# High part first in every weight-stationary stage, and two changes of place in the down-projections

## The chip, the cores and the metric

The kernel runs on 1 core of one Trainium2 chip. The metric is the device time of one execution in microseconds (us). Before the change it is 592.21 us, the median of 3 runs (592.15 to 592.26).

## The reference, cut to what matters

A decoder trunk of two layers works on one sequence of 256 positions with a width of 1024, all in float32. Layer 0 mixes with an mLSTM, layer 1 with a block-sparse attention on shared keys and values; behind each mixer stands a convolutional feed-forward block, and it is there that most of the products are:

```python
def conv_ffn(x, norm_g, w_up, conv_w, conv_b, w_down):
    u = rmsnorm(x, norm_g) @ w_up                  # 1024 -> 5632
    up = jnp.pad(u, ((0, 0), (CONV_W - 1, 0), (0, 0)))
    c = conv_b + up[:, 0:s_] * conv_w[0]
    for j in range(1, CONV_W):                     # 3 taps along the sequence
        c = c + up[:, j:j + s_] * conv_w[j]
    val, gate = jnp.split(c, 2, axis=-1)           # 2816 each
    return (jax.nn.silu(gate) * val) @ w_down      # 2816 -> 1024
```

## The kernel before, in words

Activations lie transposed: 128 channels on the partitions, 256 positions along the free axis. Every number that enters a product is split in two float32r parts, a high part `hi` (a rounded copy, made by ScalarE) and a low part `lo` (the rest, made by VectorE as raw minus `hi`). A product of x and w is taken as w_hi·x_hi + w_hi·x_lo + w_lo·x_hi.

**The weight-stationary step.** `steps_w` (L226) makes products whose weights are the stationary operand. For each k (a block of 128 input channels) it issues two matmuls into one PSUM bank: the *high* one, 128x128 weights from `hi` against 512 columns (x_hi and x_lo side by side in one tile, `both[k]`), and the *low* one, weights from `lo` against the 256 columns of x_hi. In what follows a pair of these is called a step; it has 768 columns. The order within a step is a parameter: with `order="h"` the high matmul comes first, with `order="l"` the low one does, except at k = 0. TensorE runs its instructions in the order in which the program writes them (L86); the other engines' orders are set by a planner.

**Where `steps_w` is used, in order of time.**
- `kq_steps` (L547): 8 outputs of 8 steps each, order l; the first two are taken in turns with a gate matmul (L556).
- `project_out` (L301), once a layer: 8 outputs of 8 steps, order l. The first four outputs are done in two halves of k, since the second half of the operand comes late.
- The up-projection (`pair`, L359), once a layer: 22 weight tiles (i), each with two outputs of 8 steps. Tiles 0 and 1 go ahead in turns, order l. For the others L387 chooses: layer 0, i = 2 to 11: order h, the two outputs one after the other; layer 0, i = 12 to 21: order l, in turns; layer 1, i = 2 to 11: order h, "side" (both high matmuls of a k, then both low ones); layer 1, i = 12 to 21: order h, in turns.
- The down-projection (`down`, L393), once a layer: 8 outputs of 22 steps each, 176 steps; order h in layer 0, l in layer 1. The last output of layer 1 takes its high matmul in two of 256 columns (`apart=False`).

**Weights.** `unit` (L155) loads one tile by one DMA into `raw`, and splits it in two equal pieces. `raw` has 3 buffers, `hi` and `lo` have 4 each, all of 2048 elements a partition. A tile of the up-projection holds 16 blocks of 128 columns, so the k of one output are 1024 bytes apart; a tile of the down-projection holds 11, and its k are 512 bytes apart, on end.

**Places.** Operand tiles are 2048 bytes a partition each. In the program before, those called `xa` and `xb` (the operands of all other stages) begin 1152 bytes behind a multiple of 2048, those called `f` (the 22 operands of a down-projection, made in `finish`) 256 bytes behind one. All `hi` and `lo` tiles begin 128 bytes behind a multiple of 2048. The `f` tiles are the first in their pool; four kinds of small tiles (`xs`, `y`, `sg`, `a`) lie behind them.

Of the kernel before, what the change touches and what calls it, by code (L numbers as in the profile page):

```python
# [11 lines left out]
F32 = mybir.dt.float32  # L12
# [6 lines left out]
P = 128  # L19
D = 1024  # L20
S = 256
# [48 lines left out]
def mix(steps, items=()):  # L70

    items, now = list(items), 0.0
    for cost, step in steps:
        while items and items[0][0] <= now:
            items.pop(0)[1]()
        step()
        now += cost
    for _, item in items:
        item()
# [3 lines left out]
def yoco_kernel(ctx: ExitStack, tc: tile.TileContext, A, out):  # L83
# [20 lines left out]
    @contextmanager  # L104
    def lend(label, name):
        with tc.tile_pool(name=label, bufs=2, reuse_waits="tile", space=bass.MemoryType.PSUM) as p:
            ring[name].insert(0, (p, 2))
            turns[name] = 0
            yield
            ring[name].pop(0)  # L110
            turns[name] = 0
# [43 lines left out]
    def unit(src, length, pieces=PIECES):  # L155
# [7 lines left out]
            nc.vector.tensor_tensor(lo[:, c], raw[:, c], hi[:, c].bitcast(F32), OP.subtract)  # L163
        return hi, lo

    def split(hi, lo, src, g=None):
        if g is None:
            return (nc.scalar.activation(hi, src, AF.Copy),
                    nc.vector.tensor_tensor(lo, src, hi.bitcast(F32), OP.subtract))  # L169
        return (nc.scalar.activation(hi, src, AF.Copy, scale=g),  # L170
                nc.vector.scalar_tensor_tensor(lo, src, g, hi.bitcast(F32), op0=OP.mult, op1=OP.subtract))  # L171
# [13 lines left out]
    def operand(pool, name, n):  # L185
        ts = [pool.tile([P, 2 * S], F32R, name=f"{name}{k}") for k in range(n)]
        return [t[:, :S] for t in ts], [t[:, S:] for t in ts], ts
# [35 lines left out]
            nc.scalar.activation(self.rB, pb[:, :S], AF.Copy)  # L223


    def steps_w(ps, w, at, x, ks, kall, done=None, apart=True, order="l", part="hl"):  # L226


        xh, xl, both = x

        def one(k):
            (hi, lo), p = w(), ps()
            c = slice(at(k), at(k) + P)
            last = k == kall - 1
            first = k == 0 or order == "h"

            def high():
                if not apart:
                    for n, xs in enumerate((xh, xl)):
                        nc.tensor.matmul(p[:, :S], hi[:, c], xs[k], start=k == 0 and n == 0,  # L240
                                         stop=last and not first and n == 1)
                    return
                nc.tensor.matmul(p, hi[:, c], both[k], start=k == 0, stop=last and not first)  # L243

            if first and "h" in part:
                high()
            if "l" in part:
                nc.tensor.matmul(p[:, :S], lo[:, c], xh[k], start=False, stop=last and first)  # L248
            if not first:
                high()  # L250
            if last and done is not None:
                done(p)

        return [(0.32, lambda k=k: one(k)) for k in ks]
# [37 lines left out]
    def residual(n, ps, gains, apart=True):  # L292
        nc.vector.tensor_tensor(hT[:, n], ps[:, :S], hT[:, n], OP.add)
        if apart:
            nc.vector.tensor_tensor(hT[:, n], ps[:, S:], hT[:, n], OP.add)
        if gains is None:
            nc.sync.dma_start(out[:, n, :], hT[:, n])
        else:
            feed(n, gains)
# [16 lines left out]
    def conv_ffn(l, gains):  # L316
        r = Rstd()
        with tc.tile_pool(name=f"ffn{l}", bufs=1, reuse_waits="tile") as fp, \
                tc.tile_pool(name=f"ffw{l}", bufs=2, reuse_waits="tile") as fw, lend(f"ffp{l}", "acc"):
            act = operand(fp, "f", KF)  # L320
            ah, al, _ = act

            def conv(ps, c, scaled):
                u = whole(ps)
                if not scaled:
                    nc.vector.tensor_tensor(u, u, r.rB, OP.mult)
                w = [par[:, C_CW + (l * 3 + j) * 2 * KF + c:][:, :1] for j in range(3)]
                b = par[:, C_CB + l * 2 * KF + c:][:, :1]
                y = fw.tile([P, S], F32, name="y", bufs=4)
                nc.scalar.activation(y, u, AF.Identity, bias=b, scale=w[2])  # L330
                for j in (1, 0):
                    d = 2 - j
                    nc.vector.scalar_tensor_tensor(y[:, d:], u[:, :S - d], w[j], y[:, d:],  # L333
                                                   op0=OP.mult, op1=OP.add)
                return y

            def finish(i, ps):
                y = [conv(ps[half](), half * KF + i, i >= DEFER) for half in range(2)]
                sg = fw.tile([P, S], F32, name="sg", bufs=2)
                nc.scalar.activation(sg, y[1], AF.Silu)  # L340
                a = fw.tile([P, S], F32, name="a", bufs=2)
                nc.gpsimd.tensor_tensor(out=a, in0=sg, in1=y[0], op=OP.mult)  # L342
                nc.scalar.activation(ah[i], a, AF.Copy)  # L343
                nc.gpsimd.tensor_tensor(out=al[i], in0=a, in1=ah[i].bitcast(F32), op=OP.subtract)  # L344

            def rescale():

                r.row()
                g0 = C_FNORM + l * KD
                for k in range(KD):  # L350
                    xs = fw.tile([P, S], F32, name="xs", bufs=4)
                    new = (nc.vector.scalar_tensor_tensor(xs, hT[:, k], par[:, g0 + k:g0 + k + 1], r.rB,
                                                          op0=OP.mult, op1=OP.mult),
                           nc.scalar.activation(setB[0][k], xs, AF.Copy))
                    if k == KD // 2 - 1:
                        half.extend(new)
                    nc.gpsimd.tensor_tensor(out=setB[1][k], in0=xs, in1=setB[0][k].bitcast(F32), op=OP.subtract)

            def pair(i, ks, order="l", turns=False):  # L359
                x = setA if i < DEFER else setB  # L360
                st = [steps_w(ps[i][half], w[i], lambda k, half=half: k * 256 + half * P, x, ks, KD, order=order)
                      for half in range(2)]
                if turns == "side":
                    parts = [[steps_w(ps[i][half], w[i], lambda k, half=half: k * 256 + half * P, x, ks, KD,
                                      order="h", part=part) for half in range(2)] for part in ("h", "l")]
                    return [s for k in range(len(ks)) for part in parts for s in (part[0][k], part[1][k])]
                return [s for both in zip(*st) for s in both] if turns else st[0] + st[1]


            w = [Once(lambda i=i: unit(A["w_up"][l, i], 2048)) for i in range(KF)]  # L370
            w[AHEAD] = Once(lambda: behind(last, lambda: unit(A["w_up"][l, AHEAD], 2048)))
            w[AHEAD + 1] = Once(lambda: behind(half, lambda: unit(A["w_up"][l, AHEAD + 1], 2048)))
            half = []
            ps = [[Once(acc) for half in range(2)] for i in range(KF)]


            late = []
            steps = []
            for k in range(KD):
                new = [s for i in range(AHEAD) for s in pair(i, [k])]  # L380
                steps += new[:-1] + late
                late = new[-1:]
            mix(steps + late, [(3.0, r.sums), (5.0, rescale)])
            for i in range(AHEAD):
                finish(i, ps[i])
            for i in range(AHEAD, KF):
                mix(pair(i, range(KD), *((("h", False), ("l", True)), (("h", "side"), ("h", True)))[l][i // 12]))  # L387
                finish(i, ps[i])

            wd = [Once(lambda i=i: unit(A["w_down"][l, i], 11 * P)) for i in range(2 * KD)]  # L390
            pd = [Once(acc) for n in range(KD)]

            def down(n, ks):  # L393
                apart = gains is not None or n < KD - 1
                return [s for k in ks for s in
                        steps_w(pd[n], wd[2 * n + k // 11], lambda q: (q % 11) * P, act, [k], KF,
                                lambda p: residual(n, p, gains, apart), apart, "h" if l == 0 else "l")]


            for ks in (range(KF // 2), range(KF // 2, KF)):  # L400
                for n in range(HOLD):
                    mix(down(n, ks))
            for n in range(HOLD, KD):
                mix(down(n, range(KF)))
# [509 lines left out]
```

## Time and profile before

| | |
|---|---|
| median of 3 runs | 592.21 us |
| the profiled execution's own time | 591.4 us |
| its span, first to last instruction | 589.7 us |
| TensorE busy | 583.8 us, 99% of the span |
| VectorE busy | 486.9 us, 83% |
| ScalarE busy | 393.4 us, 67% |
| GpSimd busy | 164.6 us, 28% |
| granted TensorE clock | 1.0 (the 2.4 GHz level) throughout |

The profile is of one execution. PE is TensorE's matmuls, PEld its weight loads, DVE VectorE, ACT ScalarE, POOL GpSimd. A matmul's recorded duration overlaps that of its neighbours, so the time that a matmul takes of its stage is read from one start to the next, or from the length of a stretch over the matmuls in it.

### The profile page before, as it was taken

The page shows a single profiled execution, that of the slowest core. Times are in us where ns is not written, and L with a number is a line of the kernel's source. Part 1 is how long each engine was busy: PE and PEld are TensorE (multiplying, and loading weights), DVE is VectorE, ACT ScalarE, POOL GpSimd, SP SyncE. Part 2 cuts the span into 40 slices and gives each one's busy share as a digit, 9 for nine tenths or more (in the row PEclk, how much of TensorE's full clock was granted, in tenths as well). Part 3 has the DMA queues.
Part 4 walks back from the last instruction along what each step waited for, and adds up shares of the span by engine and source line. Part 5 has one row for each costly group of instructions (what it writes and reads, how often), then busy time and mean ns, then how long its engine had stood idle before and what let it go on. Part 6 is the DMA issues. An engine that isn't in the chain of part 4 may idle for free.

```text
span 589.7 us, 9006 instructions
## 1 busy us (share of the span) xinstructions
PE 583.8 (99%) x3266; PEld 503.5 (85%) x3266; DVE 486.9 (83%) x843; ACT 393.4 (67%) x731; POOL 164.6 (28%) x178
## 2 busy tenths in 40 slices
PE   8999999999999999999999999999999999999997
PEld 5888888888888888888888888888888888888887
DVE  6888677799999998788867787577999999988550
ACT  6777776486786785775666687646887778776330
POOL 3001301352455444401211110025335343431000
PEclk9999999999999999999999999999999999999999
DMA  8657434347544544476745533333554645446720
GB/s 292 240 218 272 143 142 149 138 157 272 204 153 162 197 169 124 153 264 223 265 163 217 200 124 140 127 132 131 188 203 182 214 148 210 147 149 212 235 98 18
DMA packets 18620, 105.77 MB, mean 179 GB/s; under 512 B 2320, under 2 KB 3856, under 8 KB 9104
## 3 DMA queue, kind: packets, MB, share of 16 engines
q1 hardware_dynamic: 18288, 104.68, 49.8%
q10 hardware_dynamic: 288, 0.52, 0.3%
q8 instruction: 25, 0.41, 0.3%
q14 instruction: 19, 0.16, 0.1%
HBM read 104.15 MB, written 1.05 MB: 178 GB/s over the span
## 4 chain that ended last, share of the span: by engine, by line
PE 98%; DMA 1%; DVE 0%; SPq 0%; ACT 0%; issue 0%
PE acc L243 48%; PE acc L248 25%; PE acc L265 6%; PE acc L267 6%; PE acc L266 6%; PE acc L240 1%; DMA hT<-xT 1%; PE mis L643 1%; PE mis L761 1%; PE acc L771 1%; PE mis L815 0%; PE mis L789 0%; PE acc L770 0%; PE mis L816 0%; PE mis L675 0%; PE mis L610 0%
## 5 line engine op out<-in xcount | busy, mean ns | idle before, releaser
L163 DVE TENSOR_TENSOR lo<-raw,hi 128x1024 fp32r<-128x1024 f32 (+1 forms) x210 | 235.5, 1155 | 23.0 <-ACT hi L162 22.6
L243 PE MATMUL acc<-xb,hi 128*128 128x512 f32 x736 | 250.4, 394 | 0.0
L162 ACT ACTIVATE hi<-raw 128x1024 fp32r<-128x1024 f32 (+1 forms) x210 | 193.1, 968 | 44.2 <-PE acc L243 22.2
L248 PE MATMUL acc<-xb,lo 128*128 128x256 f32 x736 | 190.2, 279 | 0.0
L243 PEld LDWEIGHTS acc<-xb,hi 128*128 128x128 f32 x736 | 131.4, 188 | 23.6 <-DVE xb L171 0.2
L248 PEld LDWEIGHTS acc<-xb,lo 128*128 128x128 f32 x736 | 138.6, 188 | 8.4
L243 PE MATMUL acc<-f,hi 128*128 128x512 f32 x330 | 115.5, 393 | 0.0
L333 DVE SCALAR_TENSOR_TENSOR y<-whole,par,y 128x254 f32<-128x254 f32 (+1 forms) x176 | 100.3, 605 | 2.1 <-ACT y L330 1.4
L248 PE MATMUL acc<-f,lo 128*128 128x256 f32 x352 | 98.2, 283 | 0.0
L342 POOL TENSOR_TENSOR a<-sg,y 128x256 f32<-128x256 f32 x44 | 59.5, 1354 | 104.7 <-ACT sg L340 104.6
L243 PEld LDWEIGHTS acc<-f,hi 128*128 128x128 f32 x330 | 61.6, 188 | 13.7
L248 PEld LDWEIGHTS acc<-f,lo 128*128 128x128 f32 x352 | 66.1, 188 | 0.6
L330 ACT ACTIVATE y<-whole,par 128x256 f32<-128x256 f32 x88 | 51.1, 594 | 11.4 <-DVE whole L286 7.7
L243 PE MATMUL acc<-xa,hi 128*128 128x512 f32 x160 | 55.7, 395 | 1.0 <-DVE xa L171 1.0
L265 PE MATMUL acc<-hi,xa 128*128 128x512 f32 x128 | 52.6, 411 | 0.0
L344 POOL TENSOR_TENSOR f<-a,f 128x256 fp32r<-128x256 f32 x44 | 42.2, 959 | 31.3 <-ACT f L343 31.2
L267 PE MATMUL acc<-hi,xa 128*128 128x512 f32 x128 | 50.2, 392 | 0.0
L266 PE MATMUL acc<-lo,xa 128*128 128x512 f32 x128 | 50.0, 390 | 0.0
L199 POOL TENSOR_TENSOR sqacc<-sqacc,sq 128x256 f32<-128x256 f32 x18 | 16.1, 897 | 105.4 <-ACT sq L198 105.2
L248 PE MATMUL acc<-xa,lo 128*128 128x256 f32 x160 | 42.7, 284 | 0.3 <-DVE lo L169 0.3
L343 ACT ACTIVATE f<-a 128x256 fp32r<-128x256 f32 x44 | 18.2, 414 | 32.0 <-POOL a L342 32.0
L286 DVE TENSOR_TENSOR whole<-acc,whole 128x256 f32<-128x256 f32 x89 | 35.1, 413 | 3.3 <-ACT whole L285 3.3
(198 smaller groups left out, 664.4 us busy)
## 6 DMA issues: line engine op xcount, KB each, us to landing
raw<-w_up SPq DMA_DIRECT2D x44, 1024.0 KB, 4.8
raw<-w_down SPq DMA_DIRECT2D x32, 704.0 KB, 4.1
raw<-w_kqv SPq DMA_DIRECT2D x12, 1024.0 KB, 4.8
raw<-w_vo SPq DMA_DIRECT2D x8, 1024.0 KB, 5.2
raw<-w_out SPq DMA_DIRECT2D x4, 1024.0 KB, 4.7
raw<-w_o SPq DMA_DIRECT2D x4, 1024.0 KB, 4.8
raw<-w_kq SPq DMA_DIRECT2D x2, 1024.0 KB, 8.0
raw<-w_kq SPq DMA_DIRECT2D x2, 512.0 KB, 6.4
```

The costliest lines, as they stand in the source:

```text
L162: nc.scalar.activation(hi[:, c], raw[:, c], AF.Copy)
L163: nc.vector.tensor_tensor(lo[:, c], raw[:, c], hi[:, c].bitcast(F32), OP.subtract)
L243: nc.tensor.matmul(p, hi[:, c], both[k], start=k == 0, stop=last and not first)
L248: nc.tensor.matmul(p[:, :S], lo[:, c], xh[k], start=False, stop=last and first)
L265: nc.tensor.matmul(p, xh[k][:, ts], hi[:, c], start=k == 0, stop=False)
L266: nc.tensor.matmul(p, xh[k][:, ts], lo[:, c], start=False, stop=False)
L267: nc.tensor.matmul(p, xl[k][:, ts], hi[:, c], start=False, stop=k == KD - 1)
L286: nc.vector.tensor_tensor(y, ps[:, :S], y, OP.add)
L330: nc.scalar.activation(y, u, AF.Identity, bias=b, scale=w[2])
L333: nc.vector.scalar_tensor_tensor(y[:, d:], u[:, :S - d], w[j], y[:, d:], op0=OP.mult, op1=OP.add)
L342: nc.gpsimd.tensor_tensor(out=a, in0=sg, in1=y[0], op=OP.mult)
L344: nc.gpsimd.tensor_tensor(out=al[i], in0=a, in1=ah[i].bitcast(F32), op=OP.subtract)
```

## The change

`steps_w` loses the parameters `order` and `part`: the high matmul always comes first. `pair` loses its turns: the two outputs of a tile always follow each other. Layer 0 gets a tile of 224 floats (896 bytes) that nothing uses in front of the `f` tiles, so that these begin 1152 bytes behind a multiple of 2048. In layer 1 a new function `unit_down` makes the weights of the down-projection: blocks 0 to 7 of a tile go to its even places, blocks 8 to 10 to places 1, 3 and 5; consecutive k are then 1024 bytes apart, and the two pieces are of 8 and 3 blocks in place of 5.5 each.

```diff
+    def unit_down(src):
+        raw = wraw.tile([P, 2048], F32, name="raw")[:, :11 * P]
+        nc.sync.dma_start(raw, src)
+        hi, lo = (wsp.tile([P, 2048], F32R, name=nm) for nm in ("hi", "lo"))
+        for odd, a, b in ((0, 0, 8), (1, 8, 11)):
+            h, l = (w.rearrange("p (s e c) -> p s e c", s=8, e=2)[:, :b - a, odd] for w in (hi, lo))
+            r = raw.rearrange("p (s c) -> p s c", s=11)[:, a:b]
+            nc.scalar.activation(h, r, AF.Copy)
+            nc.vector.tensor_tensor(l, r, h.bitcast(F32), OP.subtract)
+        return hi, lo
...
-    def steps_w(ps, w, at, x, ks, kall, done=None, apart=True, order="l", part="hl"):
+    def steps_w(ps, w, at, x, ks, kall, done=None, apart=True):
...
-            first = k == 0 or order == "h"
-            def high():
-                ...
-            if first and "h" in part:
-                high()
-            if "l" in part:
-                nc.tensor.matmul(p[:, :S], lo[:, c], xh[k], start=False, stop=last and first)
-            if not first:
-                high()
+            if apart:
+                nc.tensor.matmul(p, hi[:, c], both[k], start=k == 0, stop=False)
+            else:
+                for n, xs in enumerate((xh, xl)):
+                    nc.tensor.matmul(p[:, :S], hi[:, c], xs[k], start=k == 0 and n == 0, stop=False)
+            nc.tensor.matmul(p[:, :S], lo[:, c], xh[k], start=False, stop=last)
...
+            if l == 0:
+                fp.tile([P, 224], F32, name="pad")
             act = operand(fp, "f", KF)
...
-                mix(pair(i, range(KD), *((("h", False), ("l", True)), (("h", "side"), ("h", True)))[l][i // 12]))
+                mix(pair(i, range(KD)))
...
-            wd = [Once(lambda i=i: unit(A["w_down"][l, i], 11 * P)) for i in range(2 * KD)]
+            even = l == 1
+            wd = [Once(lambda i=i: unit_down(A["w_down"][l, i]) if even else unit(A["w_down"][l, i], 11 * P))
+                  for i in range(2 * KD)]
+            def place(k):
+                q = k % 11
+                return (q if not even else 2 * q if q < 8 else 2 * q - 15) * P
...
-                        steps_w(pd[n], wd[2 * n + k // 11], lambda q: (q % 11) * P, act, [k], KF,
-                                lambda p: residual(n, p, gains, apart), apart, "h" if l == 0 else "l")]
+                        steps_w(pd[n], wd[2 * n + k // 11], place, act, [k], KF,
+                                lambda p: residual(n, p, gains, apart), apart)]
```

## Rows read from the trace of the kernel before

**Rows 1.** The page: span, TensorE's busy time, granted clock by slices.

```profile
span 589.7 us, 9006 instructions
PE 583.8 (99%) x3266; PEld 503.5 (85%) x3266; DVE 486.9 (83%) x843; ACT 393.4 (67%) x731; POOL 164.6 (28%) x178
...
PEclk9999999999999999999999999999999999999999
```

**Rows 2.** The page: chain that ended last, by engine and by line.

```profile
PE 98%; DMA 1%; DVE 0%; SPq 0%; ACT 0%; issue 0%
PE acc L243 48%; PE acc L248 25%; PE acc L265 6%; PE acc L267 6%; PE acc L266 6%; PE acc L240 1%; DMA hT<-xT 1%; PE mis L643 1%; PE mis L761 1%; PE acc L771 1%; PE mis L815 0%; PE mis L789 0%; PE acc L770 0%; PE mis L816 0%; PE mis L675 0%; PE mis L610 0%
```

**Rows 3.** Up-projections by stretch: window, its length, PE busy (matmuls touching it), clock, DMA.

```profile
127.86:177.78 49.92, 49.92 (x290) 1.00 0.57 208
177.78:233.74 55.96, 55.96 (x322) 1.00 0.47 165
413.12:468.87 55.75, 55.75 (x322) 1.00 0.54 190
468.87:524.33 55.46, 55.46 (x322) 1.00 0.50 176
```

**Rows 4.** Output projections (second four outputs), same view.

```profile
99.31:110.50 11.19, 11.19 (x65) 1.00 0.54 187
390.08:401.26 11.18, 11.18 (x65) 1.00 0.49 188
```

**Rows 5.** Order of time in the first stage: start, length, engine, line, idle before.

```profile
8.94 0.40 PE L556 MATMUL acc<-xa,hi 128*128 128x512 f32 x1
9.63 0.38 PE L248 MATMUL acc<-xa,lo 128*128 128x256 f32 x1 [0.29 <-DVE lo L169]
9.85 0.40 PE L243 MATMUL acc<-xa,hi 128*128 128x512 f32 x1
10.08 0.28 PE L248 MATMUL acc<-xa,lo 128*128 128x256 f32 x1
...
8.88 0.69 DVE L169 TENSOR_TENSOR lo<-raw,hi 128x512 fp32r<-128x512 f32 x1
...
8.23 0.62 ACT L168 ACTIVATE hi<-raw 128x512 fp32r<-128x512 f32 x1
```

**Rows 6.** The late operand of the first output projection, VectorE and TensorE.

```profile
94.20 0.48 DVE L171 SCALAR_TENSOR_TENSOR xb<-mis,par,xb 128x256 fp32r<-128x256 f32 x1 [0.54 <-ACT xb L170]
...
94.55 0.28 PE L248 MATMUL acc<-xb,lo 128*128 128x256 f32 x1
94.74 0.50 PE L243 MATMUL acc<-xb,hi 128*128 128x512 f32 x1
95.08 0.28 PE L248 MATMUL acc<-xb,lo 128*128 128x256 f32 x1
```

**Rows 7.** Down-projections by stretch: layer 0; layer 1 without its last output.

```profile
233.74:295.53 61.79, 61.79 (x354) 1.00 0.65 226
524.33:578.37 54.04, 54.04 (x311) 1.00 0.50 164
```

**Rows 8.** TensorE's order of time: layer 0 down-projection, then layer 1 up-projection in turns.

```profile
251.64 0.40 PE L243 MATMUL acc<-f,hi 128*128 128x512 f32 x1
251.88 0.28 PE L248 MATMUL acc<-f,lo 128*128 128x256 f32 x1
252.00 0.39 PE L243 MATMUL acc<-f,hi 128*128 128x512 f32 x1
252.22 0.28 PE L248 MATMUL acc<-f,lo 128*128 128x256 f32 x1
252.34 0.40 PE L243 MATMUL acc<-f,hi 128*128 128x512 f32 x1
252.58 0.28 PE L248 MATMUL acc<-f,lo 128*128 128x256 f32 x1
252.70 0.40 PE L243 MATMUL acc<-f,hi 128*128 128x512 f32 x1
...
502.84 0.40 PE L243 MATMUL acc<-xb,hi 128*128 128x512 f32 x1
503.07 0.28 PE L248 MATMUL acc<-xb,lo 128*128 128x256 f32 x1
503.19 0.39 PE L243 MATMUL acc<-xb,hi 128*128 128x512 f32 x1
```

**Rows 9.** Forms of the two splitting instructions on ACT and DVE, and of one strided write.

```profile
L163 DVE TENSOR_TENSOR lo<-raw,hi 128x1024 fp32r<-128x1024 f32 x146 | 180.9, 1267 | 11.3 <-ACT hi L162 10.9
L163 DVE TENSOR_TENSOR lo<-raw,hi 128x704 fp32r<-128x704 f32 x64 | 54.6, 897 | 11.7 <-ACT hi L162 11.6
L629 DVE SCALAR_TENSOR_TENSOR V<-acc,rc,V 128x512 fp32r<-128x512 f32 x4 | 3.0, 748 | 0.8 <-ACT V L628 0.8
```

**Rows 10.** Splits of two down-projection tiles, TensorE's use of them; VectorE busy.

```profile
242.70 1.70 DVE L163 TENSOR_TENSOR lo<-raw,hi 128x704 fp32r<-128x704 f32 x2 [0.20 <-ACT hi L162]
...
245.56 0.28 PE L248 MATMUL acc<-f,lo 128*128 128x256 f32 x1
...
533.90 2.23 DVE L163 TENSOR_TENSOR lo<-raw,hi 128x704 fp32r<-128x704 f32 x2
...
541.86 0.28 PE L248 MATMUL acc<-f,lo 128*128 128x256 f32 x1
...
127.86:177.78 49.92, 49.92 (x77) 1.00 0.57 208
```

**Rows 11.** Slowest step rows: layer 1's last output; two steps of layer 1's ahead tiles.

```profile
578.37:582.28 3.91, 3.91 (x34) 1.00 0.10 34
405.57:406.29 0.72, 0.72 (x6) 1.00 0.00 0
```

More of the change, by code (lines that the diff above doesn't have):

```diff
@@ L234, in one @@
             last = k == kall - 1
-            first = k == 0 or order == "h"
-            def high():
[L238 to L243, printed above, removed]
-            if first and "h" in part:
-                high()
-            if "l" in part:
-                nc.tensor.matmul(p[:, :S], lo[:, c], xh[k], start=False, stop=last and first)
-            if not first:
-                high()
+            if apart:
[4 more added lines that the diff above has]
+            nc.tensor.matmul(p[:, :S], lo[:, c], xh[k], start=False, stop=last)
             if last and done is not None:
@@ L357, in rescale, with pair @@
                     nc.gpsimd.tensor_tensor(out=setB[1][k], in0=xs, in1=setB[0][k].bitcast(F32), op=OP.subtract)
-            def pair(i, ks, order="l", turns=False):
+            def pair(i, ks):
                 x = setA if i < DEFER else setB
[L361 to L367, printed above, removed]
+                return [s for half in range(2)
+                        for s in steps_w(ps[i][half], w[i], lambda k, half=half: k * 256 + half * P, x, ks, KD)]
             w = [Once(lambda i=i: unit(A["w_up"][l, i], 2048)) for i in range(KF)]
```

## Prediction

> **What bounds the kernel now.** I read the page's busy times first: TensorE is busy for 583.8 of 589.7 us, at a granted clock of 1.0 (the 2.4 GHz level) in every slice [rows 1]. The chain of waits says the same: 98% of it is TensorE, 48% the high matmuls of the weight-stationary steps (L243) and 25% the low ones (L248) [rows 2]. So time is lost or won only in how fast matmuls follow each other, and the third view is the windows, from which the length of one step (768 columns) is worked out.
> - Up-projection, layer 0, order h, outputs one after the other: 9 tiles of 16 steps in 49.92 us, 346.7 ns a step.
> - The same, order l in turns: 10 tiles in 55.96 us, 349.8 ns.
> - Layer 1, "side": 10 tiles in 55.75 us, 348.4 ns. Order h in turns: 55.46 us, 346.6 ns [rows 3].
> - Output projections, order l: 32 steps in 11.19 and in 11.18 us, 349.5 ns [rows 4].
> - Down-projections: 176 steps in 61.79 us (order h), 351.1 ns; 154 steps in 54.04 us (order l), 350.9 ns [rows 7].
>
> The reader is to see two things. Order h has the best figure, 346.7 ns, and reaches it in turns or without. And the down-projections stand 4.3 ns above it, in either order: something else than order holds them there.
>
> **Part 1, high part first.** No instruction is added or taken away; each gain is a stretch brought down to 346.7 ns a step.
> - Layer 0, up, i = 12 to 21: 55.96 - 160 x 0.3467 = 0.49 us.
> - Layer 1, up, i = 2 to 11: 55.75 - 55.47 = 0.28 us. For i = 12 to 21 order h stays, only the turns go: 0.
> - Output projections, 64 steps: 11.19 + 11.18 - 22.19 = 0.18 us.
> - The first stage. At 9.63 us TensorE starts the low matmul of k = 2, for which VectorE makes `lo` until 9.57; behind it runs the high one, 9.85 to 10.08. Its `hi` had been there since 8.85, and TensorE had only the gate matmul of 8.94 to run [rows 5]. With the high matmul first, it runs in that wait, and 0.23 us (10.08 - 9.85) goes from the time behind 9.63. Bounds: 0, if its place in the wait is not free, and 0.33, if the low matmul, 0.22 long here and 0.12 at 10.08, shortens as well. I take 0.23.
> - All other order-l steps (the rest of the first stage, the first halves of the output projections, the ahead tiles) have waits and transposes among them; they number some 170. If each lost the 2.8 ns of rows 4, 0.5 us is there; if nothing changes, 0. I take 0.2.
> - Against it: with the high matmul first, x_lo is wanted 0.12 us earlier. The one place in the trace where it is late is the fourth k of the first output projection: VectorE ends it at 94.68, TensorE starts the high matmul at 94.74, and the low one at 94.55 had been run meanwhile [rows 6]. That cover goes: 0.1 us lost, 0.2 at most, as the low matmul is no longer than that.
>
> Sum of part 1: 0.49 + 0.28 + 0.18 + 0.23 + 0.2 - 0.1 = 1.28 us. The bounds are 0.75 (the last three at 0, 0 and -0.2) and 1.8 (at 0.33, 0.5 and 0).
>
> Without turns, the two outputs of a tile end 2.8 us apart (8 steps) in place of together, so VectorE gets its work more evenly. It is the engine to fear: in a stretch without turns it is busy for all of 49.92 us, and the lead of weights over their use falls in the layer 0 down-projection, where a tile split from 242.70 to 244.40 is used at 245.56, some 2 us behind its first piece [rows 10]. TensorE will be there about 1 us earlier by the sums above (0.49 + 0.23 + some). I cost that at 0: half the lead is left.
>
> **Part 2, layer 0's operands 896 bytes on.** No instruction changes. The row to explain is the 351.1 ns. In time order the starts of three steps go 251.64, 252.00, 252.34, 252.70: steps of 0.36, 0.34, 0.36 us, over and over [rows 8]. The period is three steps; the weights, 512 bytes on from step to step, would show a period of two if their place counted by kilobytes, and they jump from tile to tile; neither is seen. And in layer 1's up-projection in turns the weights follow each other at 512 bytes exactly as in the down-projection, yet a step takes 346.6 ns [rows 3, 8]. So the weights' stride does not look like the cause. What stays constant within each stage and differs between them is the operand's place: 1152 behind a multiple of 2048 where steps take 346.7, 256 where they take 351. The pad makes it 1152. If that is the cause, 61.79 - 176 x 0.3467 = 0.77 us goes. Bounds: a loss up to the slowest steps of rows 11 (0.72 us for two, so 0.36 each and +1.6 us), a gain of 0.77. I take 0.77, by the nearest row, the same order and place in the up-projection.
>
> A rule speaks against it. The Trainium skill (TensorE: Matmul & The Clock Gate, "Step-by-step: what each phase is for") says that TensorE has two independent SBUF read ports, one for the moving operand and one for weights, and that loading the next weights takes no read bandwidth from the running matmul. By it places would not matter, parts 2 and 3 would give 0, and the sum would be part 1's alone. The 4.3 ns between up and down in the trace are not explained by that rule.
>
> **Part 3, layer 1's weights in every other place.** By the argument of part 2 I take 0 for the place. Bounds: a gain of 54.04 - 154 x 0.3467 = 0.65 us, and 0.1 more in the last output, whose steps take 3.91 us / 11 = 355.5 ns [rows 11]; and the same loss as in part 2. The splitting work is the same 1408 elements a tile on ACT and DVE; the pieces are now 1024 and 384, so the first comes about 0.37 us later on DVE (1267 against 897 ns), and a strided write of 512 elements took 748 ns [rows 9]. Hidden by the lead of the weights: a tile whose second piece VectorE ends at 536.13 is used from it at 541.86, 5.7 us later [rows 10]; gone is that cover only if the planner puts the splits some 5 us later. The DMA of a tile and its place on SP's queue stay as they are.
>
> **Sum.** 1.28 + 0.77 + 0 = 2.05 us. On the profiled execution's own 591.4 us (1.7 beyond its span, which stay) that gives 589.35; the median shown, 592.21, stands 0.8 us above that execution, so 590.2 us.
>
> **Rivals.**
> - *Places do nothing.* Parts 2 and 3 give 0: 592.21 - 1.28 = 590.9 us. For it: `f` differs from `xb` in more than place (another part of the memory, 22 tiles in place of 8). Against it: up, down and the output projections each keep one figure all along. The skill's port rule is on this rival's side.
> - *Both changes of place work*, as a conflict between operand and weights that either one dissolves: 590.2 - 0.75 = 589.4 us. For it: it is the distance of the two that both edits change. Against it: the layer 1 rows in turns.
> - *Only the weights' place works*: the time is the forecast's within 0.1 us, 590.2, but the gain lies in layer 1.
> - *The places backfire* and the kernel is slower. Place: both down-projections; mechanism: the new distance between operand and weights, now the same for nearly every k, is a bad one for every step. For it: steps of 355.5 to 360 ns do occur [rows 11]. Price at 360 ns: 330 steps x 9 = 3.0 us, less part 1's 1.28: 593.9 us. It decides above 351 + 1.28 / 330, that is 354.9 ns a step. Against it: 1152 is where all other stages have their operand.
>
> **How the numbers follow.** Forecast 0.44; only the weights 0.08; places do nothing 0.28; both 0.13; backfire 0.07. What can be told from no change is 0.2% of the time, 1.2 us: faster means below 591.0. Forecast and its twin give that nearly always (0.50 of 0.52), both always (0.13), "nothing" in half of its cases, as part 1's bounds of 0.75 and 1.8 lie on both sides of 1.2 (0.14): faster 0.77. Backfire at its full price is slower by more than that, and a stall on VectorE adds little: 0.05. The rest, 0.18, is within 0.2%. The range goes from 589.2 (both work, part 1 somewhat better) to 591.4 (places do nothing, part 1 at its lower bound of 0.75), and leaves out backfire and the tails.
>
> **What would show it.** Right: every 16-step tile of both up-projections in 5.55 us; the layer 0 down-projection in 61.0 us with steps of 346.7 ns; layer 1's in 54.0 with 351 ns; the low matmul of k = 2 in the first stage still at 9.63, but a high one ahead of it. Wrong: TensorE idle for VectorE's `lo` about 245 us; a step of 351 in layer 0 down (then place is not it); a shorter step in layer 1 down (then the weights' place counts); an output projection above 349.5 ns.

## The result and the profile after

The changed kernel takes 595.44 us, the median of 6 runs (592.99 to 598.26); the kernel before takes 592.18 us beside it (591.61 to 593.04). The ratio is 1.0062, 95% interval 1.0046 to 1.0077: it is slower, and the forecast of 590.2 us, range 589.2 to 591.4, was wrong. The second thing to see is the spread: 5.3 us where the kernel before has 1.4.

The profiled execution is the fastest of the six, 592.99 us. Its page, the rows that answer to [rows 1, 2]:

```profile
span 591.3 us, 9025 instructions
PE 585.0 (99%) x3266; PEld 504.6 (85%) x3266; DVE 475.5 (80%) x843; ACT 392.8 (66%) x731; POOL 165.2 (28%) x178
...
PE 87%; issue 4%; DVE 4%; POOL 3%; DMA 1%; ACT 1%; SPq 0%; POOLq 0%; ACTq 0%
```

TensorE still fills 99% of the span, but the chain that ends last is no longer 98% TensorE: GpSimd (POOL) has come in, with 3%. The view of TensorE's waits (line, releaser, us in total, times, longest) says where:

```profile
PE acc L248 <- POOL xb L362: 1.1, 2, 0.6
```

Before, TensorE never waited for this line, the making of the low operand parts in `rescale`. The windows, as in [rows 3, 4, 7] (window, length, PE busy, clock, DMA), place it:

```profile
100.27:111.59 11.32, 11.32 (x67) 1.00 0.49 185
123.52:129.17 5.65, 5.65 (x35) 1.00 0.18 33
129.17:135.60 6.43, 5.86 (x35) 1.00 0.87 357
135.60:235.44 99.84, 99.84 (x579) 1.00 0.47 176
235.44:296.45 61.01, 61.01 (x354) 1.00 0.64 224
...
419.65:426.08 6.43, 5.86 (x35) 1.00 0.88 339
426.08:525.92 99.84, 99.84 (x579) 1.00 0.50 176
525.92:579.99 54.07, 54.07 (x311) 1.00 0.51 172
```

Tiles 4 to 21 of both up-projections take 99.84 us, 5.547 a tile, 346.7 ns a step: as forecast. So does layer 0's down-projection, 61.01 us. But tile 3, the first to use the scaled operand (`setB`), takes 6.43 us in both layers, tile 2 takes 5.65 in place of 5.55 (in layer 1 too), and the output projection of layer 0 is above its 11.19 [rows 4]. TensorE's order of time in tile 3 of layer 0 (start, length, instruction, idle before; the high matmul starts 0.85 us behind the low one, where 0.12 is usual, and the view counts 0.57 of that as idle):

```profile
131.52 0.28 PE L252 MATMUL acc<-xb,lo 128*128 128x256 f32 x1
132.37 0.50 PE L248 MATMUL acc<-xb,hi 128*128 128x512 f32 x1 [0.57 <-POOL xb L362]
132.70 0.28 PE L252 MATMUL acc<-xb,lo 128*128 128x256 f32 x1
```

The same program was profiled a second time (e1_again below, an execution of 597.25 us). By the starts of the stretches in the three traces:

| stretch, us | before | after | after, again |
|---|---|---|---|
| span's start to the second half of output projection 0 | 99.31 | 100.27 | 99.41 |
| second half of output projection 0 | 11.19 | 11.32 | 11.31 |
| up-projection 0, ahead tiles included | 123.24 | 123.85 | 125.82 |
| down-projection 0 | 61.79 | 61.01 | 62.20 |
| layer 1 to its output projection's second half | 94.55 | 94.59 | 94.57 |
| second half of output projection 1 | 11.18 | 11.10 | 11.09 |
| up-projection 1 | 123.07 | 123.78 | 125.77 |
| down-projection 1 and the end | 65.4 | 65.4 | 65.3 |
| span | 589.7 | 591.3 | 595.5 |

The forecast gains lie in the middle column (0.78 in the down-projection); what the change cost lies in the up-projections, and differs from one execution to the next.

### The profile page after: what moved, and what is told of

The parts are those of the page before. It is cut to its first block, busy times and chain, and to the rows that moved or that the text cites. A ratio compares the mean times of both kernels' runs of the same rounds, so it can differ in the third digit from the quotient of the medians.

```text
span 591.3 us, 9025 instructions
## 1 busy us (share of the span) xinstructions
PE 585.0 (99%) x3266; PEld 504.6 (85%) x3266; DVE 475.5 (80%) x843; ACT 392.8 (66%) x731; POOL 165.2 (28%) x178
## 4 chain that ended last, share of the span: by engine, by line
PE 87%; issue 4%; DVE 4%; POOL 3%; DMA 1%; ACT 1%; SPq 0%; POOLq 0%; ACTq 0%
PE acc L248 41%; PE acc L252 21%; PE acc L267 6%; PE acc L269 6%; PE acc L268 6%; POOL xb L362 3%; DVE lo L163 2%; DVE xa L183 1%; PE acc L251 1%; PE mis L649 1%; DMA fst<-first 1%; PE mis L767 1%; PE acc L777 1%; POOL rc L228 1%; DVE hT L295 1%
## 5 line engine op out<-in xcount | busy, mean ns | idle before, releaser
L248 PE MATMUL acc<-xb,hi 128*128 128x512 f32 x736 | 257.0, 394 | 1.2 <-POOL xb L362 1.1
L163 DVE TENSOR_TENSOR lo<-raw,hi 128x1024 fp32r<-128x1024 f32 (+1 forms) x178 | 207.5, 1193 | 15.1 <-ACT hi L162 14.4
L252 PE MATMUL acc<-xb,lo 128*128 128x256 f32 x736 | 205.1, 279 | 0.0
L162 ACT ACTIVATE hi<-raw 128x1024 fp32r<-128x1024 f32 (+1 forms) x178 | 169.2, 1000 | 33.1 <-issue 9.7
L248 PEld LDWEIGHTS acc<-xb,hi 128*128 128x128 f32 x736 | 137.9, 187 | 33.2 <-POOL xb L362 1.8
L338 DVE SCALAR_TENSOR_TENSOR y<-whole,par,y 128x255 f32<-128x255 f32 (+1 forms) x176 | 90.5, 556 | 20.2 <-ACT y L335 18.5
L347 POOL TENSOR_TENSOR a<-sg,y 128x256 f32<-128x256 f32 x44 | 63.3, 1440 | 104.1 <-ACT sg L345 103.7
L248 PE MATMUL acc<-xa,hi 128*128 128x512 f32 x160 | 59.0, 408 | 0.5 <-DVE xa L183 0.5
L349 POOL TENSOR_TENSOR f<-a,f 128x256 fp32r<-128x256 f32 x44 | 36.3, 826 | 29.7 <-ACT f L348 29.7
L248 PEld LDWEIGHTS acc<-xa,hi 128*128 128x128 f32 x160 | 30.7, 192 | 8.3 <-ACT hi L180 1.4
```

The lines of the kernel that those rows point to most:

```text
L162: nc.scalar.activation(hi[:, c], raw[:, c], AF.Copy)
L248: nc.tensor.matmul(p, hi[:, c], both[k], start=k == 0, stop=False)
```

## The experiments

Each kernel was timed against the kernel before on the same chip; ratios are against that. e1 to e4 ran on one chip (before: 591.85 us), e5 to e8 on another (591.73), e9 to e11 on a third (591.53), e12 on a fourth (591.43).

**e1_again**: the changed kernel, no edit.

> The changed kernel once more, to see what its executions have in common. Theory A (late split): the planner put two weight splits of ScalarE ahead of the last two splits of the up-projection's operand, so TensorE waits 0.8 to 0.9 us for GpSimd in tile 3 of each layer, in every execution; the rest of the spread comes from the first stage's clock. Then the trace shows both waits again (a low matmul of k = 6 of tile 3 about 0.85 us long), and a first stage that ends between 15.3 and 17 us. Theory B (VectorE overrun): some executions have waits for VectorE's splits later on; then a slower trace shows gaps in tiles 4 to 21 or in the down-projections. Time: 593 to 598 us.

596.78 us (592.19 to 597.29), 1.0066 [1.0045, 1.0088]. Its windows: tile 3, tiles 4 to 21 and the down-projection of layer 0, then tiles 4 to 21 of layer 1:

```profile
128.11:134.79 6.68, 5.87 (x35) 1.00 0.87 331
134.79:236.54 101.75, 101.75 (x578) 1.00 0.50 178
236.54:298.74 62.20, 62.20 (x355) 1.00 0.61 212
...
428.41:530.17 101.76, 101.76 (x578) 1.00 0.49 179
```

The same instructions in the same order on TensorE, no wait in any of the 18 tiles, and yet 101.75 us in place of 99.84: 353.3 ns a step. Within the stretch, tiles take 5.650, 5.650, 5.660 us, over and over; in the trace of the result it was 5.547, 5.547, 5.546. So order h has two steady rhythms. The wait in tile 3 can turn one into the other: tile 2 of layer 0 takes 5.55 us here and the tiles behind the wait 5.65, in the result's profile it is 5.65 and then 5.55. The rhythm goes over into layer 0's down-projection, which takes 62.20 us, 353.4 ns a step. All this costs 1.91 + 1.19 + 1.92 = 5.0 us against the profile of the result; the span is 4.2 us longer, mainly because its first stage is 0.9 us shorter.

**e2_pad**: the kernel before and only the 896 bytes in layer 0. **e3_wplace**: the kernel before and only layer 1's weights in every other place.

```diff
+            if l == 0:
+                fp.tile([P, 224], F32, name="pad")      # e2_pad
...
+            even = l == 1      # e3_wplace, with unit_down and place(k) as in the change
```

> Kernel before with the 896-byte pad in layer 0 alone, all orders as before. Place theory: layer 0's down-projection takes 61.0 us in place of 61.8 (346.7 ns a step), everything else as before: 0.75 us less, ratio 0.9987. Rival (the step is shortened only together with the other order changes): 61.8 us, ratio 1.000.

> Kernel before with layer 1's down-projection weights in every other place, order l kept. Place theory: the weights' place does nothing, 350.9 ns a step, layer 1's down-projection as before, ratio 1.000. Rival (splitting into strided places slows ScalarE or VectorE): splits longer than 1267 ns for 1024 elements, or a wait of TensorE; ratio above 1.001.

e2_pad: 591.30 us (590.54 to 592.29), 0.9989 [0.998, 0.9997]. e3_wplace: 592.29 us (591.28 to 593.41), 1.0005 [0.9996, 1.0014]. The layer 0 down-projection of e2_pad, then the layer 1 one of e3_wplace:

```profile
233.60:294.62 61.02, 61.02 (x353) 1.00 0.66 228
```

```profile
525.13:579.19 54.06, 54.06 (x311) 1.00 0.49 169
```

61.02 for 61.79 and 54.06 for 54.04 [rows 7]: the operands' place is worth 0.77 us, the weights' place nothing. (The small tiles behind the operands in their pool move by the same 896 bytes.)

**e4_honly**: the changed kernel without either change of place, so the high part first and nothing else.

```diff
-            if l == 0:
-                fp.tile([P, 224], F32, name="pad")
...
-            even = l == 1
+            even = False
```

> The changed kernel without the pad and with the weights in their old places: order h everywhere, no turns. Theory A: the waits of 0.85 us in tile 3 of both layers and the slower first stage are all here; both down-projections at 351 ns; 0.75 us above the changed kernel, ratio to before about 1.007, with the same spread. Rival (the places cause the loss): ratio about 0.998, as the forecast's part 1 has it.

595.22 us (593.42 to 596.12), 1.0051 [1.0036, 1.0066]. Part 1 alone makes it slower. Tiles 4 to 21 of layer 0, then of layer 1:

```profile
135.76:237.52 101.76, 101.76 (x579) 1.00 0.50 178
...
428.84:528.68 99.84, 99.84 (x578) 1.00 0.49 176
```

One layer has the slow rhythm, the other the fast one, in one execution. Its layer 0 down-projection, with the operands in their old place, takes 61.79 us behind a slow up-projection, exactly as before behind a fast one: at that place order h has the 351 ns and no second rhythm. Layer 1 of e1_again and of e5_defer4 says the same (54.07 us behind 101.76). At the new place the down-projection takes 62.20 us in the slow rhythm (e1_again), more than at the old one. The 0.75 us by which this kernel was to be slower than the changed one are not seen: its median is 1.6 us lower, and the intervals overlap.

Why the operand is late is seen in ScalarE's order. In the trace of the result (start, length, instruction):

```profile
126.20 2.01 ACT L162 ACTIVATE hi<-raw 128x1024 fp32r<-128x1024 f32 x2
...
128.36 0.74 ACT L359 ACTIVATE xb<-xs 128x256 fp32r<-128x256 f32 x2
...
128.87 3.45 POOL L362 TENSOR_TENSOR xb<-xs,xb 128x256 fp32r<-128x256 f32 x2 [3.29 <-ACT xb L359]
```

ScalarE splits two pieces of weights before it makes the last two operand copies; POOL's two subtractions begin at 128.87 and end at 132.32, when TensorE has waited since about 131.8. In the program before, one copy stands between the two pieces and one behind them (e9_ahead_l, whose order is the same, is shown below), and POOL ends at 129.15:

```profile
126.79 2.36 POOL L357 TENSOR_TENSOR xb<-xs,xb 128x256 fp32r<-128x256 f32 x2 [2.33 <-ACT xb L354]
```

The orders of the other engines are set by the planner; of the kernels here all with the ahead tiles high part first have the late order, and all others the early one.

**e5_defer4**: the changed kernel, the scaled operand used one tile later, so that it has 5.55 us more.

```diff
-DEFER = 3
+DEFER = 4
```

> The changed kernel with one number changed: four tiles of the up-projection, not three, use the operand without the gain (setA), so that the first tile on the other operand (setB) comes 5.55 us later. Theory (late operand and state): in the changed kernel ScalarE's static order puts two weight splits ahead of the last two operand copies, POOL's last operand is late, TensorE waits some 0.6 to 0.9 us in tile i = 3, and that wait leaves the matmuls in a slower steady rhythm (353 ns a step in place of 346.7) for all tiles behind it. With 5.55 us of lead the wait is gone: no tile of 6.4 us, all tiles of both up-projections 5.55 us, the layer 0 down-projection at 346.7 ns a step, layer 1's at 351; median 590.2 to 591.2 us, 5 to 6 us under the changed kernel's. Rival (order h without turns is itself unsteady, or VectorE is too late throughout): rhythm of 353 ns appears in one layer or the other without a wait, time stays at 594 to 597 us.

593.26 us (591.73 to 598.34), 1.0036 [1.0016, 1.0055]. Tiles 4 to 21 of layer 0, then tiles 2 and 3 and tiles 4 to 21 of layer 1:

```profile
133.53:233.37 99.84, 99.84 (x578) 1.00 0.50 176
411.86:423.16 11.30, 11.30 (x66) 1.00 0.53 191
423.16:524.92 101.76, 101.76 (x578) 1.00 0.50 178
```

The wait is gone in both layers, and the ratio falls from 1.0062 and 1.0066 to 1.0036, by 1.5 to 1.8 us: about what tile 3 took twice (0.88), though the intervals overlap. But the spread stays, 6.6 us, and layer 1 is in the slow rhythm from tile 2 on, without any wait. So the theory of the wait explained only part: the rhythm can be slow already when the ahead tiles hand over.

**e6_best**: the kernel before, high part first and without turns only from tile 2 on and in the down-projections, operands moved by 896 bytes in both layers.

```diff
+            fp.tile([P, 224], F32, name="pad")
             act = operand(fp, "f", KF)
...
-                mix(pair(i, range(KD), *((("h", False), ("l", True)), (("h", "side"), ("h", True)))[l][i // 12]))
+                mix(pair(i, range(KD), "h"))
...
-                                lambda p: residual(n, p, gains, apart), apart, "h" if l == 0 else "l")]
+                                lambda p: residual(n, p, gains, apart), apart, "h")]
```

> The kernel before, with the operands of the down-projection moved by 896 bytes in both layers, and the high part first without turns in the up-projection from i = 2 on and in both down-projections; the first stage, the output projections and the ahead tiles keep the order they had, layer 1's weights keep their places. Theory: ScalarE's static order of operand copies is that of the kernel before, so POOL's last operand is in time, no wait in tile i = 3, no slow rhythm: up-projections 5.55 us a tile, both down-projections at 346.7 ns a step: 0.49 + 0.28 + 0.77 + about 0.65 = 2.2 us under the kernel before, ratio 0.996. Rival (places alone matter in layer 0): layer 1's down-projection stays at 351 ns, 1.5 us, ratio 0.9975. Rival (the whole of order h is unsteady): 353 ns a step appears, 592 us or more.

590.12 us (589.64 to 590.75), 0.9971 [0.9962, 0.9981]: faster than both. Tiles 4 to 21 of layer 1, then both down-projections:

```profile
423.33:523.17 99.84, 99.84 (x578) 1.00 0.52 182
233.62:294.63 61.01, 61.01 (x354) 1.00 0.65 228
523.17:576.56 53.39, 53.39 (x311) 1.00 0.54 178
```

Every stretch has 346.7 ns a step, layer 1's down-projection too (53.39 / 154), which had 351 before and in the changed kernel. No wait in tile 3, and a spread of 1.1 us. The four stretches together are the 2.2 us shorter that were expected; the ratio shows 1.7, with 1.1 to 2.2 in its interval.

**e7_kicks**: e6_best with one small extra matmul ahead of some tiles, its output unused.

```diff
...
+                if i in kick:      # i = 5, 8, 11, 14, 17, 20; 32 to 256 columns
+                    nc.tensor.matmul(kp[:, :kick[i]], setB[0][0][:, :P], setB[0][0][:, :kick[i]], start=True, stop=True)
```

> The kernel of e6_best with one small extra matmul (of 32 to 256 columns, its output unused) ahead of the tiles i = 5, 8, 11, 14, 17, 20 in both layers: it disturbs the rhythm of the matmuls and nothing else. Theory of two steady rhythms (346.7 and 353 ns a step, whichever a disturbance leaves it in): some of the twelve kicks change the tiles behind them from 5.55 to 5.65 us, and these then stay at 5.65 us until the next kick; about 0.1 us more for each such tile. Rival (the slow rhythm needs another engine's late operand or load on the memory): every tile stays at 5.55 us, and only the extra matmuls' own 12 x 0.1 us is added.

595.02 us (two runs), 1.0055 [1.0038, 1.0072]. The kick ahead of tile 11 of layer 0 in TensorE's order of time; then, as windows, tile 9, tiles 11 and 12, tile 15:

```profile
172.87 0.28 PE L248 MATMUL acc<-xb,lo 128*128 128x256 f32 x1
172.99 0.21 PE L391 MATMUL mis<-xb 128*128 128x96 f32 x1
173.03 0.46 PE L243 MATMUL acc<-xb,hi 128*128 128x512 f32 x1
```

```profile
161.89:167.44 5.55, 5.55 (x34) 1.00 0.44 173
173.03:178.75 5.72, 5.72 (x36) 1.00 0.58 183
178.75:184.40 5.65, 5.65 (x35) 1.00 0.53 188
...
195.73:201.27 5.54, 5.54 (x34) 1.00 0.49 189
```

The third window is the tile behind the one with the kick, which has no kick of its own and takes 5.65; the kick ahead of tile 14 puts the rhythm right again (5.54). Behind six of the twelve kicks the rhythm is the fast one, behind six the slow one. Behind both layers' last kick it is the slow one, and the down-projections that follow take 62.19 and 54.42 us, 353.4 ns a step, at the place that has 346.7 in e6_best. TensorE has no wait in either up-projection, and about the kick shown (160 to 181 us) the other engines run the order that they have in e6_best: a disturbance of TensorE alone is enough, and it works in both directions.

**e8_pads** and **e11_pads2**: e6_best with other places of the operands.

```diff
-            fp.tile([P, 224], F32, name="pad")
+            fp.tile([P, (32, 96)[l]], F32, name="pad")       # e8_pads; (64, 128)[l] in e11_pads2
```

> The kernel of e6_best with the operands of the down-projection moved by 128 bytes in layer 0 and 384 bytes in layer 1, in place of 896, so that they stand 384 and 640 behind a multiple of 2048 (256 in the kernel before, 1152 with 896). Weights stand 128 behind a multiple of 512. Theory (a certain place, 1152): both down-projections at 351 ns a step. Theory (distance between operand and weights a multiple of 512): layer 0 at 351, layer 1 at 346.7. Theory (an odd multiple of 128): both at 346.7.

> The kernel of e6_best with the operands of the down-projection moved by 256 bytes in layer 0 and 512 in layer 1, so that they stand 512 and 768 behind a multiple of 2048: even multiples of 128, as the 256 of the kernel before; 384, 640 and 1152, the places that took 346.7 ns a step, are odd ones. Theory (odd or even multiple of 128 decides): both down-projections at 351 ns a step. Rival (256 alone is a bad place): both at 346.7. Third (a multiple of 512 is a place of its own): layer 0 differs from layer 1.

e8_pads: 589.14 us (589.00 to 590.40, 4 runs), 0.9963 [0.9949, 0.9977]. e11_pads2: 591.19 us (590.27 to 591.68), 0.999 [0.998, 1.0]. The down-projections of e8_pads, then of e11_pads2:

```profile
233.10:294.12 61.02, 61.02 (x355) 1.00 0.67 228
522.66:576.04 53.38, 53.38 (x310) 1.00 0.55 178
```

```profile
233.49:295.27 61.78, 61.78 (x354) 1.00 0.67 226
523.77:577.82 54.05, 54.05 (x310) 1.00 0.52 176
```

At 384, 640 and 1152 bytes behind a multiple of 2048 (odd multiples of 128) a step takes 346.7 ns, at 256, 512 and 768 (even ones) 351. Weights stood 128 behind a multiple of 512 throughout; whether the operand's place counts by itself or by its distance to them was not tried.

**e9_ahead_l**: the changed kernel, only the two ahead tiles low part first. **e10_ahead_h**: e6_best, only these tiles high part first.

```diff
...
-                new = [s for i in range(AHEAD) for s in pair(i, [k])]
+                new = [s for i in range(AHEAD) for s in pair(i, [k], "l")]     # e9_ahead_l; "h" in e10_ahead_h
```

> The changed kernel with one thing undone: the two ahead tiles of each up-projection (i = 0 and 1, whose steps lie among transposes) have the low part first again; all else is as changed. ScalarE's static order of operand copies is then that of the kernel before. Theory (the ahead tiles are the cause of both losses: the late operand in tile i = 3, and the slow rhythm in which they hand over to the tiles behind them): no wait in tile 3, 5.55 us a tile in both up-projections in the trace, layer 0 down at 346.7 ns a step, layer 1 at 351; median 590.5 to 591.0 us (0.7 above e6_best for layer 1's down-projection), lowest to highest within 1.5 us. Rival (order h everywhere else is at fault too, by the first stage or the output projections): the spread of 592 to 598 stays, median above 593.

> The kernel of e6_best with one thing added: the two ahead tiles high part first. Theory (as in e9_ahead_l): this alone brings back the wait of about 0.9 us in tile i = 3 of each layer and, in some executions, the rhythm of 353 ns: median 592.5 to 595.5 us, spread 592 to 597. Rival (the ahead tiles do no harm by themselves): 590.1 us as e6_best, no wait.

e9_ahead_l: 589.85 us (589.73 to 590.29), 0.9968 [0.9956, 0.998]. e10_ahead_h: 595.03 us (591.41 to 598.80), 1.0068 [1.0047, 1.0089]. One parameter of two tiles in each layer carries the whole loss, taken away or brought back; without it the change has about the ratio that was forecast for it (590.2 / 592.21 = 0.9966). ScalarE's and POOL's order in e9_ahead_l:

```profile
125.41 1.07 ACT L162 ACTIVATE hi<-raw 128x1024 fp32r<-128x1024 f32 x1
126.36 0.43 ACT L363 ACTIVATE xb<-xs 128x256 fp32r<-128x256 f32 x1
126.67 1.07 ACT L162 ACTIVATE hi<-raw 128x1024 fp32r<-128x1024 f32 x1
127.62 0.42 ACT L363 ACTIVATE xb<-xs 128x256 fp32r<-128x256 f32 x1
...
126.86 2.35 POOL L366 TENSOR_TENSOR xb<-xs,xb 128x256 fp32r<-128x256 f32 x2 [2.35 <-ACT xb L363]
```

POOL ends at 129.21; TensorE wants the last operand at 122.37 + 5.55 + 7 x 0.347 = 130.35. In the result's profile, where tile 2 begins 1.15 us later (123.52), it ends 3.1 us later. Tiles 2 to 21 of layer 0 in e9_ahead_l (layer 1: 110.94), then tile 2, tile 3 and the rest of layer 0 in e10_ahead_h:

```profile
122.37:233.32 110.95, 110.95 (x642) 1.00 0.50 178
```

```profile
122.30:127.95 5.65, 5.65 (x35) 1.00 0.17 41
127.95:134.37 6.42, 5.86 (x34) 1.00 0.89 324
134.37:234.21 99.84, 99.84 (x578) 1.00 0.49 176
```

**e12_final**: e9_ahead_l with the operands of layer 1 moved as well and its weights back in their old places.

> The kernel of e9_ahead_l with the operands of the down-projection moved by 896 bytes in layer 1 too, and layer 1's weights back in their old places: high part first everywhere but in the ahead tiles. Theory: layer 1's down-projection goes from 351 to 346.7 ns a step, 154 x 4.3 = 0.66 us, all else as in e9_ahead_l (0.9968 of the kernel before): median 0.9957 of the kernel before, some 589.2 us, below both kernels. Rival (the unequal pieces of layer 1's weights had hidden something): no gain against e9_ahead_l, 0.9968.

589.93 us (588.93 to 590.74), 0.9967 [0.9953, 0.9982]. Its layer 1 down-projection takes what was expected:

```profile
522.49:575.87 53.38, 53.38 (x310) 1.00 0.54 178
```

The 0.68 us are in the trace (54.06 in e9_ahead_l), but not in the ratio, whose interval is 1.7 us wide; the spread that is left, 1.8 us, may come in part from the stages ahead of the second half of the first output projection, which starts between 98.99 and 99.69 us in the traces of the four kernels named next. e6_best, e8_pads, e9_ahead_l and e12_final can't be told apart by their ratios; all beat both kernels.

## Why the prediction was wrong

- **Up-projections, 0.49 and 0.28.** Right in size for tiles 4 to 21 of the result's profile, and in full in e9_ahead_l: 110.95 us for 320 steps.
- **Part 2, 0.77; part 3, 0.** Right: e2_pad and e3_wplace, alone. *Only the weights' place* and *both work* fall by e3_wplace, *backfire* by both. *Places do nothing* falls by e2_pad. The Trainium skill's rule of two independent read ports ("TensorE: Matmul & The Clock Gate", "Step-by-step: what each phase is for") gave that last rival; the trace goes against what was drawn from it: with nothing but the operands' place changed, a step takes 346.7 or 351 ns.
- **"All other order-l steps ... I take 0.2", the ahead tiles among them.** This is the step that failed. I bounded it by 0 below and priced the ahead tiles as steps to be shortened; they are a place where a planner's order and a rhythm are decided. By e9_ahead_l against the changed kernel, and e10_ahead_h against e6_best, order h in these tiles costs 0.9 to 1.0%, 5.6 and 5.7 us. Two things are in it. First, with order h there, ScalarE's order puts the last two operand copies behind two splits, and TensorE waits in tile 3: 6.43 for 5.55 us, twice 0.88. The lead that this ate was 1.1 us (129.21 to 130.35 in e9_ahead_l, whose order is that of before), and it could have been read from the trace before (129.15, and 127.86 + 7 x 0.347 = 130.29). Second, the rhythm, which is slow or fast by execution. In the traces with the ahead tiles in order h, tile 2 has the slow rhythm in 7 of 10 layers (five traces), and tile 4, behind the wait, in 3 of 8; with order l there and order h from tile 2 on, tiles 2 and 3 have the fast one in 15 of 15 layers. Only profiled executions show their rhythm; that it also makes the spread of the others is inferred.
- **The 346.7 ns as a property of order h.** This premise failed with it: e1_again shows 353.3 for the same instructions. The sum took one mean for each stretch [rows 3, 4], 346.7 as order h's figure and 349.5 as order l's. But the trace before already has both rhythms, in order l. Here are the second and third of the four outputs of [rows 4], 8 steps each:

```profile
102.09:104.91 2.82, 2.82 (x18) 1.00 0.78 270
104.91:107.69 2.78, 2.78 (x18) 1.00 0.86 256
```

In the first of them the high matmuls start 0.36, 0.35 and 0.35 us apart, over and over, as in the slow rhythm of e1_again; in the second 0.350 and 0.343 in turn, 346.7 ns on the mean. The outputs alternate so in both layers, and 349.5 ns is a mean of the two. Layer 1's ahead tiles, order l too, have the slow rhythm ahead of two small matmuls at 407.34 us (the two steps of [rows 11] are of it) and 346.7 ns a step from 408.73 to 413.12. So "the output projections each keep one figure all along", said against *places do nothing*, was a misreading; and what order h gains in such a stage is that a change of output does not change the rhythm.
- **"VectorE ... is the engine to fear".** Wrong engine in the place that was named: no wait for VectorE's `lo` appears about 245 us, and the layer 0 down-projection ran at full pace. POOL, busy for 28%, was late by an order that ScalarE was given.
- **Output projections, 0.18.** Half right: layer 1's goes to 11.10, layer 0's to 11.32 and 11.31. The late x_lo was priced at 0.1, 0.2 at most; it comes (in the result's profile the high matmul starts 0.31 us behind the low one of 95.27, in place of 0.12), but what costs is the slow rhythm behind it: 353 ns a step for the 32 steps that follow, in all six traces with order h there.
- **The first stage, 0.23.** The step does what was forecast [rows 5]: in e1_again the high matmul of k = 2 runs in the wait and the low one starts at 9.61 behind it.

```profile
9.17 0.40 PE L248 MATMUL acc<-xa,hi 128*128 128x512 f32 x1
9.61 0.39 PE L252 MATMUL acc<-xa,lo 128*128 128x256 f32 x1
```

The next two outputs begin at 15.04 there, at 15.33 before. But they then take 5.86 in place of 5.57 us, and both traces are at 20.90 behind them: in e1_again the weights of the low matmul of 16.86 wait 0.34 us for a `lo` that VectorE ends at 16.81, so the gain was given back to VectorE. In e12_final, where the two outputs take 5.56, it is 20.48. Up to 99 us the traces with order h there (98.99 to 100.34) can't be told from those with order l (99.13 to 100.11). In the result's profile the first stage ran late for another reason, the clock. At 9.65 us a high matmul starts 0.43 us ahead of the next one in place of 0.23, the pace of the lower level (1.2 GHz). The view reads 1.00 there only because it counts time without a clock record as full: the record of this trace begins at 10.47 us, with 1.0, and from 10.61 on the pace is 0.23. It begins at 10.11 us in e4_honly, which has the same slow matmuls, and between 4.06 and 6.74 in the twelve other traces (6.25 before, 5.46 in e1_again). In e11_pads2, where it begins at 4.06, the first matmuls of the program, all alike, go from 0.43 to 0.22 us apart just there. In the result's profile TensorE had run ten matmuls, stood idle from 5.70 to 6.25 us and run twelve more before the rise; why it came later in two of the traces is open.

Open as well: what makes the two rhythms, which of the ahead tiles' changes (TensorE's own order or the planner's) hands over the slow one, and why the planner's order turns on these tiles; for the rhythms the runs show only when they change.

## What to carry to other kernels

Where TensorE is busy for 99%, a stage's time a step is no constant of its instructions: before taking a stretch's best figure for the rest, read the stretch output by output, and in several executions, for a second figure, and widen the range by the difference. When an edit reorders instructions ahead of a planner, read the orders that the other engines get, and above all the last operand to arrive: an edit that costs nothing on its own engine can move a copy on another. Undo the edit at the seams between stages first; here the whole gain was to be had with the two tiles among the transposes left as they were.

## What the runs showed that was not expected

- A chain of matmuls of 512 and 256 columns in turn has two steady rhythms, 346.7 and 353.3 ns a step; a wait of 0.6 us or one matmul of 96 columns changes from one to the other, and it then stays for 18 tiles and a down-projection, until the next disturbance. In order l the output projections change rhythm with every output (2.78 and 2.82 us), which is what their 349.5 ns a step is made of.
- The place of the moving operand modulo 256 bytes (six places tried) is worth 4.3 ns of 351 a step (1.2%), in order h; with the operand at the even place the second rhythm does not appear behind a slow up-projection (three stages).
- POOL's two subtractions of 128x256 take 3.45 us where VectorE's splits run beside them for 2.9 us of it, 2.36 and 2.35 in the early order, with splits for 0.9; that these are the cause was not tested by itself.
